# Six longer weight buffers and a sliding start for the split weights of the gate stage

## The chip, the core and the metric

The kernel runs on one core of one Trainium2 chip. The metric is the device time of one execution in microseconds (us), as the median of several executions. One more execution was taken by the hardware profiler; all rows below are from it. Engines are named as the profile names them: PE is the matrix engine (TensorE), PEld its weight loads, DVE the vector engine, ACT the scalar engine, POOL and SP the two others, of which SP issues most transfers.

## The reference, cut to what matters

```python
h = einsum('bsd,dn->bsn', x, w_in) + b_in      # x: 1 x 512 x 2048, w_in: 2048 x 11528, float32
# columns of h: three attention branches' q, k, v, z ... and three merge gates of 2048 columns each
br_i = einsum('bsw,wd->bsd', merged_heads(o_i) * silu(z_i), w_br_i)     # i = fox, swa, moba; w = 512
y = sum_i sigmoid(gate_i) * br_i
out = einsum('bsd,de->bse', y, w_out)
x = layer_norm(2 ** 0.25 * x + out, ln_g, ln_b)
```

## The kernel before, in words

Every float32 matrix product is done as three products of float32r parts: an operand `a` is split into `hi` (a rounded copy) and `lo` (what is left of it), and `hi*hi`, `hi*lo` and `lo*hi` are added up in PSUM. The input x is split once into `xh` and `xl`, which stay in the on-chip memory. The weights come through one stream of blocks of 128 x 512 numbers, in the order of the list `ids` of `weight_stream`. A block's kind is "h" (128 columns of the projection by a quarter of the 2048 inputs; four blocks make one column tile `t`), "v", "b" (a 512 x 128 piece of a branch matrix) or "o" (a piece of the output matrix). Two blocks come in one transfer into `raw`, which SP issues.

The main loop takes one block at each step `i`. It first calls `prepare(i + 2)`, which has ACT write the block's `hi`, and at once or a little later DVE its `lo` (`lower`), two steps ahead of their use. Then it calls the step of the block's kind, which issues its matmuls, and then the tasks that were set down for this step, in a written order. `tc.manual_schedule()` keeps the engines' instructions in the order in which the code issues them. A step of kind "h" or "b" issues 12 matmuls of 512 columns each. `hi` and `lo` have three buffers each in the pool `stage`, shared by all kinds of blocks; a buffer is written again when the matmuls of the block that was there are done.

The gate stage is the loop over `dt` from 0 to 15 in `weight_stream`: three column tiles for the next `dt` (12 blocks "h", 144 matmuls, `proj_step`), then three blocks "b" (36 matmuls, `branch_step`). Column tiles 33 to 80 are the 48 of the gates; the first three of them come before the loop and those of `dt` 1 to 15 inside it. In the blocks "h" and "b" the part `hi` or `lo` is the weight side of the matmul (128 columns of it are loaded into the array), and `xh`, `xl`, `ozh` or `ozl` the side that streams through. In the blocks "o" it is the other way round: `yh` or `yl` is loaded, and `hi` or `lo` streams.

Where things lie in the on-chip memory, in bytes from the start of a partition's row, by the built program (the part of 512 is what is left over from a multiple of 512):

| tiles | part of 512 |
|---|---|
| `hi`, `lo` (all six), `xh`, `xl`, `ozh`, `ozl`, `yh`, `yl` | 480 |
| `wh`, `wl` (the parts of the last eight blocks "o") | 416 |
| `qs`, `kh`, `kl`, `lt`, `pth`, `ptl`, `ident`, `tri`, `pair` (attention) | 160 |
| `vfox`, `vswa`, `vmoba` | 32 |

The matmuls take slices of them that begin at multiples of 128 or 256 numbers, 512 or 1024 bytes. So every place at which a matmul of this kernel begins to read, other than in the warm-up, has one of these four parts of 512, and all four are 32 past a multiple of 64.

Of the kernel before, what the change touches and what calls it, by code (L numbers as in the profile page):

```python
# [9 lines left out]
F32R = mybir.dt.float32r  # L10
# [3 lines left out]
P = 128  # L14
S = 512
# [5 lines left out]
ALPHA = 2.0 ** 0.25  # L21
LN_EPS = 1e-5
WARM = 7

FOX_Q, FOX_K, FOX_V, FOX_Z, FOX_F = 0, 512, 1024, 1536, 2048
SWA_Q, SWA_K, SWA_V, SWA_Z = 2056, 2568, 2696, 2824
# [27 lines left out]
def weight_stream():  # L54

    ids = []
    t = 0

    def proj(n):
        nonlocal t  # L60
        for _ in range(n):
            ids.extend(("h", t, c) for c in range(4))
            t += 1

    proj(12)
    proj(1)
    for p in range(4):
        proj(2)
        if p % 2 == 1:
            ids.extend(("v", p // 2, g) for g in range(8))  # L70
    proj(12)
    proj(3)
    for dt in range(KD):
        if dt + 1 < KD:
            proj(3)
        ids.extend(("b", dt, b) for b in range(3))
    ids.extend(("o", ec, k) for ec in range(4) for k in range(KD))
    return ids
# [3 lines left out]
def hybrid_kernel(ctx: ExitStack, tc: tile.TileContext, a: dict, out: bass.AP):  # L82
# [16 lines left out]
    def att_tile(name):  # L99
        return psum.tile([P, S], F32, tag="att", name=name, bufs=5)  # L100
# [6 lines left out]
    ids = weight_stream()  # L107
# [7 lines left out]
    def load(j):  # L115
        if 2 * j < len(ids) and j not in raws:
            raws[j] = stage.tile([P, 1024], F32, tag="raw", name="raw", bufs=raw_bufs)
            nc.sync.dma_start(raws[j], a["ws"][j])

    def prepare(i):  # L120

        if i >= len(ids) or i in parts:
            return None
        load(i // 2)
        raw = raws[i // 2][:, (i % 2) * S:(i % 2 + 1) * S]
        if i in held:
            hi, lo = held[i]
        else:
            hi = stage.tile([P, S], F32R, tag="hi", name="hi")
            lo = stage.tile([P, S], F32R, tag="lo", name="lo")  # L130
        parts[i] = (hi, lo)
        nc.scalar.activation(hi, raw, AF.Copy)  # L132

        def lower():
            nc.vector.tensor_sub(lo, raw, hi.bitcast(F32))  # L135
            for d in range(1, raw_bufs):
                load(i // 2 + d)

        return lower
# [48 lines left out]
    wacc = att_tile("warm")  # L188
    for n in range(WARM):
        nc.tensor.matmul(wacc, warm[:, :P], warm, start=True, stop=True)  # L190
# [89 lines left out]
    for n in range(2 * KD):  # L280
        if n + 4 < KD:
            load_x(n + 4)
        if n % 2 == 0 and n // 2 + 3 < KD:
            load_v(n // 2 + 3)
        if n + 2 < 2 * KD:
            prepare_v(n + 2)
        else:
            prepare(n + 2 - 2 * KD)()
        if n == KD:
            vacc[1] = [att_tile(f"vc{i}") for i in range(4)]  # L290
        v_step(n)
        if n == 4:
            nc.vector.tensor_scalar(nsink, sinkc, -1.0, None, op0=ALU.mult)
        if KD + 1 <= n < KD + 5:
            v_evac(0, n - KD - 1, fox_dests[0])
# [270 lines left out]
    box = {}  # L566
# [174 lines left out]
    for i in range(len(ids)):  # L741
        assert i in parts
        lower = prepare(i + 2)
        if lower:
            at(i, 2, lower)
        step[ids[i][0]](i)
        for _, _, f, args in sorted(tasks.pop(i, ()), key=lambda x: x[:2]):
            f(*args)
# [69 lines left out]
```

## Time and profile before

| | |
|---|---|
| median of 3 executions | 1400.79 us (1400.56 to 1402.41) |
| the profiled execution | 1399.89 us |
| its span, from the first to the last instruction | 1398.1 us |
| PE busy | 1377.4 us, 99% of the span, 6659 matmuls |
| PEld busy | 1162.8 us, 83% |
| DVE, ACT, POOL busy | 636.3, 556.8, 151.4 us |
| mean granted clock of PE | 0.995 of 2.4 GHz |

Busy times are shares of the span over all stages. PE's matmuls overlap in the profile: one of 512 columns is shown with 389 ns, while the next begins some 227 ns after it, so the distance from start to start (the pitch) is what counts, and it is read from stretches with a known number of matmuls.

### The profile page before, as it was taken

The page shows a single profiled execution, that of the slowest core. Times are in us where ns is not written, and L with a number is a line of the kernel's source. Part 1 is how long each engine was busy: PE and PEld are TensorE (multiplying, and loading weights), DVE is VectorE, ACT ScalarE, POOL GpSimd, SP SyncE. Part 2 cuts the span into 40 slices and gives each one's busy share as a digit, 9 for nine tenths or more (in the row PEclk, how much of TensorE's full clock was granted, in tenths as well). Part 3 has the DMA queues.
Part 4 walks back from the last instruction along what each step waited for, and adds up shares of the span by engine and source line. Part 5 has one row for each costly group of instructions (what it writes and reads, how often), then busy time and mean ns, then how long its engine had stood idle before and what let it go on. Part 6 is the DMA issues. An engine that isn't in the chain of part 4 may idle for free.

```text
span 1398.1 us, 17708 instructions
## 1 busy us (share of the span) xinstructions
PE 1377.4 (99%) x6659; PEld 1162.8 (83%) x6659; DVE 636.3 (46%) x1273; ACT 556.8 (40%) x1024; POOL 151.4 (11%) x216
## 2 busy tenths in 40 slices
PE   9999999999999999999999999999999999999994
PEld 8988888898988888888888888888888888888884
DVE  5466656545554555452333333233333323733348
ACT  5355566555545566642222222222222222422231
POOL 1002122332321222100000000000000000000006
PEclk9999999999999999999999999999999999999998
DMA  7333223222223222233332333323333332363323
GB/s 245 116 105 105 83 90 89 77 88 89 82 75 91 78 76 89 76 94 102 90 106 91 101 95 94 103 90 106 91 99 97 93 103 91 122 255 98 98 75 121
DMA packets 41157, 142.37 MB, mean 102 GB/s; under 512 B 4632, under 2 KB 5144, under 8 KB 40304
## 3 DMA queue, kind: packets, MB, share of 16 engines
q1 hardware_dynamic: 40048, 134.58, 30.8%
q0 software_dynamic: 1024, 6.67, 1.3%
q8 instruction: 52, 0.85, 0.3%
q14 instruction: 33, 0.27, 0.1%
HBM read 137.02 MB, written 4.21 MB: 101 GB/s over the span
## 4 chain that ended last, share of the span: by engine, by line
PE 96%; DVE 2%; DMA 1%; SPq 0%; issue 0%; ACT 0%; DVEq 0%; ACTq 0%
PE h L471 21%; PE h L473 21%; PE h L472 21%; PE br L599 9%; PE o L651 4%; PE o L650 4%; PE o L652 4%; PE o L417 2%; PE pt L398 2%; PE mv L490 1%; PE mv L492 1%; PE mv L493 1%; PE s L357 1%; PE s L356 1%; DMA xraw<-in_xT 1%; PE vc L274 1%
## 5 line engine op out<-in xcount | busy, mean ns | idle before, releaser
L132 ACT ACTIVATE hi<-raw 128x512 fp32r<-128x512 f32 x444 | 280.1, 631 | 711.1 <-PE h L472 426.8
L135 DVE TENSOR_TENSOR lo<-raw,hi 128x512 fp32r<-128x512 f32 x444 | 313.1, 706 | 540.9 <-ACT hi L132 532.7
L471 PE MATMUL h<-xh,hi 128*128 128x512 f32 x1296 | 507.4, 392 | 0.0
L473 PE MATMUL h<-xh,lo 128*128 128x512 f32 x1296 | 505.1, 390 | 0.1
L472 PE MATMUL h<-xl,hi 128*128 128x512 f32 x1296 | 505.2, 390 | 0.0
L473 PEld LDWEIGHTS h<-xh,lo 128*128 128x128 f32 x1296 | 243.3, 188 | 52.3 <-DVE lo L135 0.5
L471 PEld LDWEIGHTS h<-xh,hi 128*128 128x128 f32 x1296 | 243.4, 188 | 48.5
L472 PEld LDWEIGHTS h<-xl,hi 128*128 128x128 f32 x1296 | 243.5, 188 | 47.9
L393 POOL TENSOR_SCALAR lt<-lt,st 128x128 f32<-128x128 f32 (+2 forms) x96 | 71.2, 742 | 302.0 <-DVE st L392 300.0
L651 PE MATMUL o<-hi,yl 128*128 128x512 f32 (+1 forms) x232 | 88.6, 382 | 0.0
L650 PE MATMUL o<-hi,yh 128*128 128x512 f32 (+1 forms) x232 | 88.6, 382 | 0.0
L652 PE MATMUL o<-lo,yh 128*128 128x512 f32 (+1 forms) x232 | 88.6, 382 | 0.0
L599 PE MATMUL br<-ozh,hi 128*128 128x512 f32 x192 | 74.7, 389 | 0.0
L599 PE MATMUL br<-ozl,hi 128*128 128x512 f32 x192 | 74.7, 389 | 0.0
L599 PE MATMUL br<-ozh,lo 128*128 128x512 f32 x192 | 74.7, 389 | 0.0
L631 POOL DMA_DIRECT2D z<-in_xn x4 | 2.2, 556 | 625.3 <-DVE yl L104 625.3
L387 ACT ACTIVATE lt<-lt,st 128x128 f32<-128x128 f32 (+3 forms) x96 | 51.4, 535 | 23.7 <-DVE st L392 10.5
L650 PEld LDWEIGHTS o<-hi,yh 128*128 128x128 f32 x232 | 43.6, 188 | 8.6
L652 PEld LDWEIGHTS o<-lo,yh 128*128 128x128 f32 x232 | 43.6, 188 | 8.5
L651 PEld LDWEIGHTS o<-hi,yl 128*128 128x128 f32 x232 | 43.6, 188 | 8.3
L405 ACT ACTIVATE pth<-pt 128x128 fp32r<-128x128 f32 (+2 forms) x96 | 38.8, 404 | 14.8 <-PE pt L398 14.0
L409 DVE TENSOR_TENSOR ptl<-pt,pth 128x128 fp32r<-128x128 f32 (+2 forms) x96 | 43.2, 450 | 1.0 <-ACT pth L405 0.7
(156 smaller groups left out, 1426.9 us busy)
## 6 DMA issues: line engine op xcount, KB each, us to landing
raw<-in_ws SPq DMA_DIRECT2D x226, 512.0 KB, 3.6
rawv<-in_wv SPq DMA_DIRECT2D x15, 324.0 KB, 4.0
xraw<-in_xT SPq DMA_DIRECT2D x16, 256.0 KB, 6.3
z<-in_xn POOLq DMA_DIRECT2D x4, 1024.0 KB, 10.1
out<-z SPq DMA_DIRECT2D x7, 512.0 KB, 2.6
row<-forget_rows SPq DMA_DIRECT2D x8, 256.0 KB, 4.0
ln_gain<-in_ln_gain POOLq DMA_DIRECT2D x1, 1024.0 KB, 18.0
ln_bias<-in_ln_bias POOLq DMA_DIRECT2D x1, 1024.0 KB, 20.4
```

Of the source, the lines that this page charges most:

```text
L132: nc.scalar.activation(hi, raw, AF.Copy)
L135: nc.vector.tensor_sub(lo, raw, hi.bitcast(F32))
L387: nc.scalar.activation(full[:, :m], full[:, :m], AF.Exp, bias=st[:, 0:1], scale=-1.0, accum_out=st[:, 1:2])
L393: nc.gpsimd.tensor_scalar(lt, lt, st[:, 3:4], 1.0, op0=ALU.mult, op1=ALU.mult)
L409: nc.vector.tensor_sub(env["ptl"][:, c], u["pt"][:, :u["n"] // P], env["pth"][:, c].bitcast(F32))
L471: nc.tensor.matmul(accs[t], hi[:, cc], xh[:, k], start=(k == 0), stop=False)
L472: nc.tensor.matmul(accs[t], hi[:, cc], xl[:, k], start=False, stop=False)
L473: nc.tensor.matmul(accs[t], lo[:, cc], xh[:, k], start=False, stop=(k == KD - 1))
L599: nc.tensor.matmul(br, w[:, cc], o[:, 4 * b + kt], start=(kt == 0 and n == 0), stop=(kt == 3 and n == 2))
L650: nc.tensor.matmul(o, yb["h"][:, k, sl], hi, start=(k == 0), stop=False)
L651: nc.tensor.matmul(o, yb["l"][:, k, sl], hi, start=False, stop=False)
L652: nc.tensor.matmul(o, yb["h"][:, k, sl], lo, start=False, stop=(k == KD - 1))
```

## The change

From the column tile 39 on, that is in `dt` 2 to 15, the blocks "h" take their `hi` and `lo` from six buffers of their own (`ghi`, `glo`, three each) in the pool `mix`. Each is 640 numbers long, and the part of 512 numbers begins `o` numbers into it. `o` is the next number of `PLACES` after every three column tiles, so each of the 14 numbers holds for one `dt`, for 12 blocks and 144 matmuls. The blocks "b", "o" and the earlier blocks "h" keep the old buffers.

```diff
+PLACES = (0, 4, 8, 12, 16, 24, 32, 48, 64, 80, 96, 112, 124, 126)
...
         if i in held:
             hi, lo = held[i]
+        elif ids[i][0] == "h" and ids[i][1] >= 39:
+            o = PLACES[min((ids[i][1] - 39) // 3, len(PLACES) - 1)]
+            hi = box["mix"].tile([P, S + P], F32R, tag="ghi", name="ghi", bufs=3)[:, o:o + S]
+            lo = box["mix"].tile([P, S + P], F32R, tag="glo", name="glo", bufs=3)[:, o:o + S]
         else:
             hi = stage.tile([P, S], F32R, tag="hi", name="hi")
```

In the built program all six new buffers lie at the part 480 of 512, as the old ones do. With 4 bytes a number the 14 starts, as parts of 512, are 480, 496, 0, 16, 32, 64, 96, 160, 224, 288, 352, 416, 464 and 472. The two last `y` tiles (`dt` 14 and 15) move 15,360 bytes up in the pool, at the same part of 512.

Every engine has the same instructions in the same order before and after. What differs beside the addresses is what some of them wait for. On ACT, where the blocks of `dt` 2 begin and the first blocks "b" after them, each row being one instruction with the queues that it waits for (DVE and PE stand for the buffer's last users, DMAHW for the transfer into `raw`), it is before:

```order
L584 ACTIVATE sig<-h_6094,bT 128x512 [waits PE_49]
L132 ACTIVATE hi<-raw 128x512 [waits DVE_49,PE_49]
L132 ACTIVATE hi<-raw 128x512 [waits DMAHW4_49,DVE_49,PE_49]
L132 ACTIVATE hi<-raw 128x512 [waits DVE_49,PE_49]
L132 ACTIVATE hi<-raw 128x512 [waits DMAHW5_49,DVE_49,PE_49]
```

and with the change:

```order
L590 ACTIVATE sig<-h_6094,bT 128x512 [waits PE_49]
L138 ACTIVATE ghi<-raw 128x512
L138 ACTIVATE ghi<-raw 128x512 [waits DMAHW4_49]
L138 ACTIVATE ghi<-raw 128x512
L138 ACTIVATE ghi<-raw 128x512 [waits DMAHW5_49,DVE_49,PE_49]
```

The first three blocks "h" and the three blocks "b" of each of the 14 `dt` no longer wait for PE (84 instructions); the nine others of each `dt` wait as before.

## Rows read from the trace of the kernel before

**Rows 1.** The page: busy us (share of the span) and instructions; the chain that ended last.
```profile
PE 1377.4 (99%) x6659; PEld 1162.8 (83%) x6659; DVE 636.3 (46%) x1273; ACT 556.8 (40%) x1024; POOL 151.4 (11%) x216
...
PE 96%; DVE 2%; DMA 1%; SPq 0%; issue 0%; ACT 0%; DVEq 0%; ACTq 0%
```

**Rows 2.** All waits of PE in the whole span: us in total, times, longest.
```profile
PE warm L190 <- DVE warm L187: 1.5, 1, 1.5
PE va L272 <- ACT xh L103: 0.8, 1, 0.8
PE va L273 <- DVE xl L104: 0.6, 2, 0.3
```

**Rows 3.** The chain that ended last, in the gate stage: start, us, what.
```profile
618.01 8.16 PE br L599 x36
658.81 8.16 PE br L599 x36
...
1148.41 8.16 PE br L599 x36
1189.21 16.32 PE br L599 x72
```

**Rows 4.** Windows: one stretch of 144 projection matmuls (two more overlap its edges): engines, clock, DMA.
```profile
626.17:658.81 32.64, 32.64 (x146) 27.04 (x145) 9.62 (x14) 8.74 (x15) 0.00 (x0) 1.00 0.33 97
```

**Rows 5.** Groups by line and shape, 658.81 to 699.61: busy us, mean ns, idle before.
```profile
L473 PE MATMUL h<-xh,lo 128*128 128x512 f32 x49 | 19.1, 389 | 0.0
...
L471 PEld LDWEIGHTS h<-xh,hi 128*128 128x128 f32 x48 | 9.0, 188 | 1.9
```

**Rows 6.** Timeline of PE, 127.5 to 131, around an attention head's values: start, us.
```profile
128.33 0.39 PE L472 MATMUL h<-xl,hi 128*128 128x512 f32 x1
128.55 0.39 PE L473 MATMUL h<-xh,lo 128*128 128x512 f32 x1
128.78 0.39 PE L417 MATMUL o<-pth,vfox 128*128 128x512 f32 x1
129.01 0.39 PE L417 MATMUL o<-ptl,vfox 128*128 128x512 f32 x1
...
129.82 0.22 PE L417 MATMUL o<-pth,vfox 128*128 128x128 f32 x1
129.88 0.28 PE L417 MATMUL o<-ptl,vfox 128*128 128x128 f32 x1
129.99 0.41 PE L398 MATMUL pt<-ident,lt 128*128 128x128 f32 x2
```

**Rows 7.** The same stretch, weight loads.
```profile
128.56 0.19 PEld L417 LDWEIGHTS o<-pth,vfox 128*128 128x128 f32 x1
```

**Rows 8.** Groups by line and shape over the whole span, output blocks streaming `hi` or `wh`.
```profile
L650 PE MATMUL o<-hi,yh 128*128 128x512 f32 x216 | 84.1, 389 | 0.0
...
L650 PE MATMUL o<-wh,yh 128*128 128x512 f32 x24 | 9.5, 394 | 0.0
```

**Rows 9.** Timeline of PE near the end: first and last of 25 output matmuls streaming `wh` or `wl`.
```profile
1358.38 0.40 PE L651 MATMUL o<-wh,yl 128*128 128x512 f32 x1
...
1363.98 0.39 PE L651 MATMUL o<-wh,yl 128*128 128x512 f32 x1
```

**Rows 10.** Timelines of ACT and of DVE, 650 to 662; idle before, and what ended it.
```profile
650.46 0.63 ACT L132 ACTIVATE hi<-raw 128x512 fp32r<-128x512 f32 x1 [1.51 <-PE h L472]
653.18 0.63 ACT L132 ACTIVATE hi<-raw 128x512 fp32r<-128x512 f32 x1 [2.09 <-PE h L472]
...
651.13 0.69 DVE L135 TENSOR_TENSOR lo<-raw,hi 128x512 fp32r<-128x512 f32 x1 [2.03 <-ACT hi L132]
```

**Rows 11.** Waits of ACT, 620 to 1189: us in total, times, longest.
```profile
ACT hi L132 <- PE h L472: 315.8, 159, 2.1
ACT hi L132 <- PE br L599: 65.0, 35, 2.1
```

## The prediction

> **What bounds the kernel now.** I read the page first. PE is busy for 1377.4 us of the 1398.1 us span, and the chain that ended last runs over PE for 96% of it [rows 1]. So the next question is whether PE ever waits for data. The list of PE's waits has three entries, 2.9 us together, all of them at the start (the warm-up and the first value blocks) [rows 2]. In the gate stage PE waits for nothing. The chain shows how regular it is: a group of 36 branch matmuls begins every 40.80 us, from 618.01 to 1148.41, thirteen periods one after the other [rows 3]. Each group takes 8.16 us, 226.7 ns for a matmul. The other 32.64 us of a period are the 144 projection matmuls, again 226.7 ns each, at a granted clock of 1.00 [rows 3, 4]. The stage's time is therefore the number of matmuls times the pitch, and nothing else. An edit moves the time here only if it moves the pitch or makes PE wait. The first of the 14 stretches that the change touches is the one of rows 4.
>
> **The removed waits.** In each of the 14 periods six blocks get their buffer without waiting for PE, so ACT and DVE can write them earlier. ACT did wait long for PE, 315.8 us and 65.0 us in this stage [rows 11], but that was the pace PE set, not a delay to PE: PE's own list has no wait there [rows 2]. There is nothing to win: 0 us. A loss would need ACT or DVE to be late. A block's `hi` is written at 650.46 and its `lo` ends at 651.13 + 0.69 = 651.82 [rows 10]. The wait before that `hi` ended with PE's last use of the buffer, so the step in progress had just begun, and the block is used two steps later. Steps are 2.72 us apart (12 matmuls, and the distance of the two ACT rows), so it is needed at about 655.9 and has 4.1 us to spare. The instructions that now carry a wait of their own (the products of branch and gate on DVE) waited for the same matmuls before, through the write of `lo` ahead of them in DVE's queue. Cost 0.
>
> **Writing to the new places.** ACT and DVE write 168 `hi` and 168 `lo` at the 14 starts. No row shows a write to a place off a multiple of 32 bytes, so I bound it: below, no change; above, twice the time, another 0.63 us on ACT and 0.69 us on DVE [rows 10]. Both together, 1.3 us, lie within the 4.1 us, so both ends cost 0. Without that cover, 14 x 12 blocks at 1.3 us would be 220 us, but the cover would have to shrink by two thirds first.
>
> **Loading weights from the new places.** This is the one term that can count, since it multiplies 14 x 144 = 2016 matmuls. A weight load is shown with 188 ns [rows 5] and runs while the matmul before it streams, so it has the 226.7 ns of the pitch. How much of this does it need? Two matmuls of 128 columns in the attention stage start at 129.82 and 129.88, and the next instruction starts at 129.99, each with a load of its own [rows 6]: 85 ns each on average, at most 110 ns. So a load that took twice as long (at most 220 ns of throughput) would still fit under the pitch. Lower bound 0, and 0 also for a load up to twice as slow.
>
> Loads may also disturb the stream that runs beside them. Addresses do matter for the streaming side: the output matmuls that stream `wh` from the part 416 of 512 are shown with 394 ns, those that stream `hi` from 480 with 389 ns, with the same weights' places [rows 8]. Read by starts, 24 pitches take 1363.98 - 1358.38 = 5.60 us, 233.3 ns each [rows 9], against 226.7 ns. A place can thus cost a step of 6.7 ns. But the change leaves the stream (`xh`, `xl` at 480) where it is and moves the loaded side. The trace has a few cases of just that. Where a projection matmul is followed by one of an attention head, the load that runs beside the projection matmul comes from `vfox`, at the part 32, rather than from 480 [rows 7]. That projection matmul starts at 128.55 and the next at 128.78, after one from 128.33 to 128.55 with a load from 480 [rows 6]: 0.22 and 0.23 us, the same to the view's 0.01 us. A step of 6.7 ns would hardly show in that one pair, which is why this evidence is good and not final. I take 0.
>
> Eight of the 14 starts (480, 32, 96, 160, 224, 288, 352, 416) are 32 past a multiple of 64, as every operand of the kernel before. Two (0 and 64) are multiples of 64, and four (496, 16, 464, 472) are off every multiple of 32: no row shows a matmul that reads at such a place, so for these six I have only the bound of one step, 6.7 ns, either way, and keep it for the range.
>
> **The sum.** 0 + 0 + 0: the profiled execution's 1399.89 us would stay. It lies 0.9 us (0.06%) below the median of the three runs, and I forecast that median, 1400.8 us. A measurement of this kernel can tell about 0.2% (2.8 us) from no change.
>
> **Rivals.**
>
> *Slower: starts off 32 bytes cost a step.* Place: the periods of 496, 16, 464 and 472. Price: 4 x 144 x 6.7 ns = 3.8 us, 1404.6 us. For it: the step exists on the streaming side [rows 8, 9], and a row of weights that straddles one more unit of the memory needs one more read. Against it: the extra read falls on the load, which has over 100 ns to spare. It decides from 4.9 ns a matmul on (2.8 us over 576). If instead all 13 moved starts cost a step, it is 13 x 144 x 6.7 ns = 12.5 us, 1413.3 us; the pair above speaks against it. Worse than a step would need a load of more than twice its time.
>
> *Faster: the start at 480 costs PE something, and other starts give it back.* 512 columns at 2.4 GHz are 213.3 ns, so 13.3 ns of each pitch are not streaming. If part of this came from loading at 480, the six unseen kinds of start could return a step each: 6 x 144 x 6.7 ns = 5.8 us, 1395.0 us; all 13 would return 12.5 us, 1388.3 us. Only the two multiples of 64 would be 1.9 us, too little to measure. For it: the excess is there, and it has the size of two steps. Against it: with a load from 32 the pitch was not shorter [rows 6].
>
> The Trainium skill ("TensorE: Matmul & The Clock Gate", section "Back-to-back issue gap") gives the warm gap as N/2.4 + 2.5 ns, 215.8 ns for 512 columns, which is 10.9 ns under what the row here shows. By that rule, taken as what well-placed operands reach, 13 moved starts could give back 13 x 144 x 10.9 ns = 20 us (an estimate from that page); the trace does not bear this out, since no 512-column matmul in it comes near that gap, from any of the four parts of 512.
>
> *The change does not do what it says.* The starts are not spread from a multiple of 512 but from 480 past one; the list of places already takes this in. It changes which starts are odd ones, not the sum.
>
> **How the numbers follow.** No measurable change 0.70: the load is hidden and eight of 14 starts are of the kind known; this holds the case of the two multiples of 64 alone. Slower 0.17: four starts cost a step 0.12, more than that 0.05. Faster 0.13: up to six starts return a step 0.09, more 0.04. The range reaches to both measured-step cases and a little beyond, 1395 to 1405 us, and leaves out about 1 in 10 by these cases, and some more for their sizes.
>
> **What would show it.** In the profile after, the branch groups should still begin 40.80 us apart in all 14 periods, and the projection groups show 389 ns. Since each period has one start, a period that is longer by 144 steps (0.96 us) names the start that costs; a shorter one names a start that pays. ACT's waits for PE in this stage should fall by some 84 entries with no new wait on PE. I am wrong if periods differ from each other, above all those of 0, 64 and of the four odd starts, or if a wait appears on PE.

## The result and the profile after

| | before | with the change |
|---|---|---|
| median | 1400.67 us (1400.27 to 1402.41) | 1408.63 us (1408.20 to 1408.97) |
| span of the profiled execution | 1398.1 us | 1406.5 us |

The change makes the kernel slower: ratio 1.0054, 95% interval 1.0037 to 1.0072. The forecast was no change, with a range that ended at 1405 us.

The page of the changed kernel: busy time by engine, and four groups by line.

```profile
PE 1386.4 (99%) x6659; PEld 1164.4 (83%) x6659; DVE 633.7 (45%) x1273; ACT 549.1 (39%) x1024; POOL 151.4 (11%) x216
...
L141 DVE TENSOR_TENSOR glo<-raw,ghi 128x512 fp32r<-128x512 f32 x168 | 116.1, 691 | 343.8 <-ACT ghi L138 343.8
...
L477 PE MATMUL h<-xh,ghi 128*128 128x512 f32 x672 | 264.2, 393 | 0.0
...
L138 ACT ACTIVATE ghi<-raw 128x512 fp32r<-128x512 f32 x168 | 103.0, 630 | 341.2 <-PE h L478 341.2
L477 PEld LDWEIGHTS h<-xh,ghi 128*128 128x128 f32 x672 | 126.4, 188 | 28.9
```

PE is busy 9.0 us longer with the same 6659 matmuls. The writes to the odd places take 630 ns on ACT and 691 ns on DVE, as before. A weight load is shown with 188 ns, as in [rows 5]. Only the matmuls beside these loads are longer: 393 ns on the mean instead of 389. PE's list of waits again has three entries, all at the start:

```profile
PE warm L196 <- DVE warm L193: 1.5, 1, 1.5
PE va L278 <- ACT xh L105: 0.7, 1, 0.7
PE va L279 <- DVE xl L106: 0.3, 1, 0.3
```

ACT's list, from 620 to 1198 us, is shorter than in [rows 11], where `hi` waits 194 times for PE:

```profile
ACT ghi L138 <- PE h L478: 341.2, 126, 8.5
ACT sig L590 <- PE h L479: 88.8, 14, 6.5
```

None of this holds PE up, so the time is in the pitch. The chain that ended last shows in which groups (start, us, what), against the even 40.80 us of [rows 3]:

```profile
618.14 8.16 PE br L605 x36
658.94 8.16 PE br L605 x36
699.74 8.17 PE br L605 x36
741.50 8.17 PE br L605 x36
783.26 8.16 PE br L605 x36
825.02 8.19 PE br L605 x36
866.95 8.17 PE br L605 x36
908.58 8.16 PE br L605 x36
949.71 8.16 PE br L605 x36
990.50 8.16 PE br L605 x36
1032.26 8.20 PE br L605 x36
1073.93 8.16 PE br L605 x36
1115.05 8.16 PE br L605 x36
1155.85 8.17 PE br L605 x36
1197.62 16.34 PE br L605 x72
```

From one row's end to the next row's start lie the 144 projection matmuls with one of the 14 starts, in the order of the list: the first from 626.30 to 658.94 (480), the third from 707.91 to 741.50 (0), and so on. 33.59 us / 144 = 233.3 ns. From the first row to the last it is 579.48 us, against 571.20 us in [rows 3]: 8.28 us of the 8.4 us by which the span grew. The windows of the groups with the starts 0 and 32 show all else as in [rows 4], the clock at 1.00 too:

```profile
707.91:741.50 33.59, 33.59 (x145) 27.05 (x145) 9.43 (x14) 8.42 (x14) 0.00 (x0) 1.00 0.34 110
791.42:825.02 33.60, 33.60 (x146) 27.07 (x145) 9.41 (x14) 8.41 (x14) 0.00 (x0) 1.00 0.36 110
```

By start (part of 512), from the starts of the matmuls in the trace, the pitch in ns:

| 480 | 496 | 0 | 16 | 32 | 64 | 96 | 160 | 224 | 288 | 352 | 416 | 464 | 472 |
|---|---|---|---|---|---|---|---|---|---|---|---|---|---|
| 226.7 | 226.7 | 233.3 | 233.3 | 233.3 | 234.2 | 232.4 | 228.9 | 226.7 | 233.3 | 232.4 | 228.9 | 226.7 | 233.3 |

Pairs that lie 256 apart (32 and 288, 96 and 352, 160 and 416, 224 and 480) agree to 0.02 ns. The pitch hangs on the start within 256 bytes, and not on whether it is a multiple of 32 or 64. Times 144, the excess over 226.67 ns adds up to 8.17 us.

### The profile page after: what moved, and what is told of

Same layout as the page of the kernel before. It is cut to its first block, busy times and chain, and to the rows that moved or that the text cites. A ratio compares the mean times of both kernels' runs of the same rounds, so it can differ in the third digit from the quotient of the medians.

```text
span 1406.5 us, 17608 instructions
## 1 busy us (share of the span) xinstructions
PE 1386.4 (99%) x6659; PEld 1164.4 (83%) x6659; DVE 633.7 (45%) x1273; ACT 549.1 (39%) x1024; POOL 151.4 (11%) x216
## 4 chain that ended last, share of the span: by engine, by line
PE 96%; DVE 2%; DMA 0%; issue 0%; ACT 0%; SPq 0%; DVEq 0%; ACTq 0%
PE h L477 21%; PE h L478 21%; PE h L479 21%; PE br L605 9%; PE o L657 4%; PE o L656 4%; PE o L658 4%; PE o L423 2%; PE pt L404 2%; PE mv L496 1%; PE mv L498 1%; PE mv L499 1%; PE s L363 1%; PE s L362 1%; PE vc L279 1%; PE vc L278 1%
## 5 line engine op out<-in xcount | busy, mean ns | idle before, releaser
L478 PE MATMUL h<-xl,ghi 128*128 128x512 f32 x672 | 264.4, 393 | 0.0
L477 PE MATMUL h<-xh,ghi 128*128 128x512 f32 x672 | 264.2, 393 | 0.0
L479 PE MATMUL h<-xh,glo 128*128 128x512 f32 x672 | 263.8, 393 | 0.0
L477 PE MATMUL h<-xh,hi 128*128 128x512 f32 x624 | 246.1, 394 | 0.0
L478 PE MATMUL h<-xl,hi 128*128 128x512 f32 x624 | 243.8, 391 | 0.0
L479 PE MATMUL h<-xh,lo 128*128 128x512 f32 x624 | 243.7, 391 | 0.1
L477 PEld LDWEIGHTS h<-xh,ghi 128*128 128x128 f32 x672 | 126.4, 188 | 28.9
L479 PEld LDWEIGHTS h<-xh,glo 128*128 128x128 f32 x672 | 126.4, 188 | 28.8
L478 PEld LDWEIGHTS h<-xl,ghi 128*128 128x128 f32 x672 | 126.4, 188 | 28.2
L477 PEld LDWEIGHTS h<-xh,hi 128*128 128x128 f32 x624 | 117.2, 188 | 22.3
```

What stands on the lines that cost most here:

```text
L477: nc.tensor.matmul(accs[t], hi[:, cc], xh[:, k], start=(k == 0), stop=False)
L478: nc.tensor.matmul(accs[t], hi[:, cc], xl[:, k], start=False, stop=False)
L479: nc.tensor.matmul(accs[t], lo[:, cc], xh[:, k], start=False, stop=(k == KD - 1))
```

## The experiments

All are edits of the changed kernel unless said otherwise. A run for which no ratio is given is a single execution; the pitches of its groups are what counts there. "Distance" is the start of the loaded weights less the start of the streamed operand, as part of 256. With the change `xh` and `xl` begin at 224 of 256, so the start 480 has distance 0, and the start 32 has distance 64.

**The buffers without the sliding start.**
```diff
-PLACES = (0, 4, 8, 12, 16, 24, 32, 48, 64, 80, 96, 112, 124, 126)
+PLACES = (0,) * 14
```


> The six new buffers stay, but all 14 starts are o = 0, the part 480 of 512. If the time hangs on where the loaded weights start (A), every projection group of the gate stage is back at 144 x 226.7 ns = 32.64 us and the time is that of before, 1400.7 us. If the new buffers themselves, their place in the memory or the waits that changed cost the time (B), it stays near 1408.6 us.

1400.29 us against 1400.71 us, ratio 0.9997 (0.9988 to 1.0006). The branch groups stand 40.80 us apart again (start and us):

```profile
618.16 8.16 PE br L605 x36
658.96 8.16 PE br L605 x36
```

So the new buffers, their place far up in the memory, the moved `y` tiles and the waits that went away are worth nothing that shows, as A had it; B falls.

**One slow start for all.** `PLACES = (24,) * 14`.

> All 14 starts are o = 24, the part 64 of 512, the start whose group was the longest with the change (33.73 us, 234.2 ns a matmul). If each start has its own price whatever came before it (A), the 2016 matmuls cost 7.57 ns each more than before: 15.3 us, 1416.0 us. If the price comes from changing the start, or depends on the group before (C), it is well below that, by the 14 changes no more than the 8 us of the change.

1415.28 us, ratio 1.0105 (1.0088 to 1.0122); A had 1416.0, C no more than 1409. All 14 groups have 234.2 ns (from branch group to branch group, start and us):

```profile
617.92 8.16 PE br L605 x36
659.81 8.16 PE br L605 x36
701.70 8.16 PE br L605 x36
```

The first gap is 659.81 - 626.08 = 33.73 us. A start has a price of its own and keeps it.

**The streamed side moved by 64 bytes.** `xh` and `xl` get a longer tile each and begin 16 numbers into it; the outputs' `yh` and `yl`, in the same two tiles, begin at 0.
```diff
-    xh = keep.tile([P, KD, S], F32R, tag="bigh", name="xh")
-    xl = keep.tile([P, KD, S], F32R, tag="bigl", name="xl")
+    def big(tag, name, o):
+        flat = keep.tile([P, KD * S + 64], F32R, tag=tag, name=name)
+        return flat[:, o:o + KD * S].rearrange("p (k s) -> p k s", s=S)
+
+    xh, xl = big("bigh", "xh", 16), big("bigl", "xl", 16)
...
+            yb["h"], yb["l"] = big("bigh", "yh", 0), big("bigl", "yl", 0)
```


> The changed kernel with its 14 starts, and the streamed xh and xl begin 64 bytes later: at the part 32 instead of 224 of 256. If the price hangs on the loaded side's start alone (theory L), or on the writes to it, the 14 groups show the same pitches as with the change: 226.7 ns at 480, 496, 224, 352+112 and 233.3 at 0, 16, 32, 288, 472. If it hangs on the distance from the streamed side's start to the loaded side's within 256 bytes (theory D), the pitches move by 64 bytes: 226.7 ns at 32 and 288 (distance 0) and 16 (distance 240), 233.3 at 64, 96 and 352 (distances 32, 64), 232 to 234 at 160 and 416 (distance 128), 228.9 at 480 and 224 (distance 192).

Its chain, from the branch group before the start 16 to the one after the start 64:

```profile
743.73 8.20 PE br L608 x36
784.60 8.17 PE br L608 x36
825.45 8.18 PE br L608 x36
867.21 8.17 PE br L608 x36
```

The group at 16 takes 784.60 - 751.93 = 32.67 us (226.9 ns; it was 233.3), the one at 32 takes 825.45 - 792.77 = 32.68 us (227.0; it was 233.3), the one at 64 takes 33.58 us (233.2). The group at 480, the good place until now, has 229.0 ns. The fast starts moved along with the stream, as D said, with nothing changed in the loads or in the writes of ACT and DVE. L falls. The total, 1409.55 us, tells little of this: the 14 starts for the most part exchanged their prices.

**More distances, and two repeated.** `PLACES = (20, 28, 36, 40, 44, 52, 56, 60, 1, 2, 3, 6, 24, 48)`.

> The changed kernel with other numbers in the list: o = 20, 28, 36, 40, 44, 52, 56, 60 (new multiples of 16 bytes: the parts 48, 80, 112, 128, 144, 176, 192, 208 of 256), 1, 2, 3, 6 (4, 8, 12 and 24 bytes past 480), and again 24 and 48. By both theories the multiples of 16 fall on the curve of the change: 233.3 at 48, 232 to 235 from 80 to 144, below 228.9 from 176 on, 226.7 at 208; 24 and 48 repeat 234.2 and 228.9 ns at another place in the order. If an odd start costs by itself, as 472 seems to, the starts 4, 8, 12 and 24 bytes past 480 show 233 ns although 480 and 496 show 226.7; if only the distance counts, they show 226.7.

The total is 1408.99 us. 24 and 48 repeat 234.2 and 228.9 ns at another place in the order. The expected curve was missed at five of the eight new multiples of 16, though, as it is no smooth one: distance 144 has 226.7 ns between 128 with 232.4 and 160 with 233.3; 208 has 231.8 and 240 has 226.7. Neither of the two values named for starts off 16 bytes, 233 for all or 226.7 for all, came out: such a start has no price as such, since 12 bytes past 480 shows 226.7 ns, but 4, 8 and 24 past show 232.4, 230.7 and 231.1.

**Only `lo` at the odd starts.**
```diff
-            hi = box["mix"].tile([P, S + P], F32R, tag="ghi", name="ghi", bufs=3)[:, o:o + S]
+            hi = box["mix"].tile([P, S + P], F32R, tag="ghi", name="ghi", bufs=3)[:, :S]
```


> The changed kernel with its 14 starts for lo alone; hi stays at o = 0. Only one load of three then comes from another distance. If the matmul that streams while such a load runs pays (D1), the one from xl and hi (line 478) is longer at the bad starts, by about 7 ns on the mean of its pitch, and the two others stay at 227 ns: a third of the 8.2 us, 2.7 us, 1403.4 us. If the matmul that uses the weights so loaded pays (D2), it is the one from lo (line 479). If the price needs a run of loads at the same distance (D3), as a settled rhythm would, all three stay at 227 ns and the time at 1400.7 us.

1407.22 us: none of the three. One odd load of three keeps most of the price. The group with `lo` at the start 32 stands between these rows of the chain:

```profile
783.33 8.16 PE br L605 x36
824.77 8.17 PE br L605 x36
```

824.77 - 791.49 = 33.28 us, 231.1 ns a matmul against 233.3 with both parts there, and from the starts in the trace the three kinds of matmul have 228, 229 and 236 ns. Which of the three pays most changes with the start: at 0 they have 232, 239 and 229 ns, at 64 233, 230 and 233. At 160 and 416 (distance 192) the one odd load costs even more than all three did, 231.1 against 228.9 ns. So the price can't be put on one matmul of the three, nor added up load by load; it looks like a rhythm of the row of matmuls as a whole.

**The kernel before with the streamed side at other places** (the edit of the 64 bytes, on the kernel before, with 28, 4 and 60 numbers for 16): an attempt to keep the gate stage and to speed up the value stages.

> The kernel before with xh and xl 112 bytes later. The projection groups load at distance 144, which showed 226.7 ns: no change there, 32.64 us a group. The 384 matmuls of 256 columns that load xh or xl and stream hi or lo (120.8 ns on the mean) and the 384 of 324 columns then work at distance 112. If the price goes by distance there too, they move: 113 to 122 ns for 256 columns, at best 384 x 7 ns = 2.7 us less (1398 us), at worst 1.5 us and for 324 columns 3 us more. If only 512-column matmuls have it, 1400.7 us.

> The kernel before with xh and xl 16 bytes later. Projection groups at distance 240 (226.7 ns, 32.64 us a group); the matmuls of 256 and 324 columns at distance 16. By distance: 113 to 122 ns for 256 columns, the time between 1398 and 1402 us; if only 512-column matmuls have the price, 1400.7 us.

> The kernel before with xh and xl 240 bytes later, the mirror of 16 bytes later: projection groups at distance 16 (226.7 ns), matmuls of 256 and 324 columns at distance 240. By distance: 113 to 122 ns for 256 columns, the time between 1398 and 1402 us; if only 512-column matmuls have the price, 1400.7 us.

1415.29, 1416.09 and 1423.18 us: ratios 1.0104 (1.0089 to 1.0120), 1.0110 (1.0093 to 1.0127) and 1.0162 (1.0146 to 1.0177). Their projection groups have 231.0, 231.7 and 233.3 ns in place of 226.7, so the distances 144, 240 and 16 weren't safe ones. The value matmuls of 256 columns gained little or nothing (121.0, 119.7 and 119.9 ns on the mean, 120.8 before). The rule of distance as stated fell here, and the next four runs ask what it lacks.

**The stream at two more multiples of 32.** The edit of the 64 bytes with 32 numbers (128 bytes), and with 8 numbers (32 bytes) and `PLACES = (8, 12, 16, 20, 24, 32, 40, 44, 48, 56, 60, 0, 4, 10)`.

> The changed kernel with its 14 starts, and xh and xl 128 bytes later, at the part 96 of 256 (32 past a multiple of 64, as in all runs in which the distance alone gave the pitch). If the distance within 256 bytes decides for such a stream, the pitches are known beforehand: 226.7 ns at 96 and 352 (distance 0) and 496 (144), 228.9 at 32 and 288 (192), 230.0 at 16 (176), 232.4 at 480 and 224 (128), 233.3 at 64 (224), at 160 and 416 (64) and at 464 (112). If the loaded side's start decides, the 14 are those of the change.

> The changed kernel with xh and xl 32 bytes later, at a multiple of 256, and other starts in the list, at the distances 0, 16, 32, 48, 64, 96, 128, 144, 160, 192, 208, 224, 240 and 8. If the distance alone decides, the pitches are, in this order, 226.7, 226.7, 233.3, 233.3, 233.3, 234.2, 232.4, 226.7, unknown, 228.9, 231.8, 233.3, 226.7 and 230.7 ns. If the stream's own start within 64 bytes counts as well, as the runs with xh and xl 16, 112 and 240 bytes later speak for, several of the 14 differ by more than 1 ns; a pitch below 226.7 ns, should there be one, would be a place for a faster kernel.

Pitches in ns by distance, from the starts of the matmuls, for the runs in which the stream begins at a multiple of 32 ("entered slow" is the run below):

| distance | change, stream at 224 | further starts, 224 | +64 bytes, at 32 | +128 bytes, at 96 | +32 bytes, at 0 | entered slow, 224 |
|---|---|---|---|---|---|---|
| 0 | 226.7 | | 227.0 | 226.7 | 226.9 | 226.9 |
| 32 | 233.3 | | 233.3 | | 233.2 | |
| 64 | 233.3 | | 233.4 | 233.3 | 233.4 | |
| 96 | 234.2 | 234.2 | | | 234.2 | |
| 128 | 232.4 | | 232.4 | 233.3 | 233.3 | |
| 192 | 228.9 | 228.9 | 229.0 | 229.0 | 228.9 | |
| 208 | | 231.8 | 231.8 | | 231.9 | |
| 224 | | 233.3 | 233.3 | 233.3 | 233.4 | |
| 12 | | 226.7 | | | | 233.3 |
| 16 | 226.7 | | | | 233.4 | 233.3 |
| 144 | | 226.7 | | 233.3 | 233.3 | 233.3 |
| 240 | 226.7 | 226.7 | 226.9 | | 228.4 | 228.4 |

Seven of the twelve are firm within 0.3 ns at each of these streams at which they were run, 128 within 1 ns. So are four that the table leaves out, each seen in two or three of these runs: 48, 112 and 160 (233.3 to 233.4 ns) and 176 (230.0). 12, 16, 144 and 240 have two values each. The slow one at 144, with the stream at 96, stands between these rows of its chain (711.12 - 677.52 = 33.60 us, 233.3 ns a matmul):

```profile
669.35 8.17 PE br L608 x36
711.12 8.19 PE br L608 x36
```

The totals, 1418.58 and 1419.58 us, are higher than that of the change for the most part because the earlier projection matmuls leave distance 0 there too: the first of the 14 groups begins 9.5 and 8.6 us later (635.60 and 634.74 us against 626.14).

**The groups entered out of a slow rhythm.** `PLACES = (0, 4, 36, 60, 0, 4, 36, 60, 3, 0, 4, 36, 60, 3)`, all 226.7 ns until now, and the branch blocks from slow starts of the same buffers, while `xh` and `xl` stay where they were:
```diff
-        elif ids[i][0] == "h" and ids[i][1] >= 39:
-            o = PLACES[min((ids[i][1] - 39) // 3, len(PLACES) - 1)]
+        elif ids[i][0] == "h" and ids[i][1] >= 39 or ids[i][0] == "b" and ids[i][1] >= 1:
+            o = (24 if ids[i][1] < 8 else 16) if ids[i][0] == "b" else PLACES[min((ids[i][1] - 39) // 3, 13)]
```


> The changed kernel with the starts o = 0, 4, 36, 60 and 3 alone, the distances 0, 16, 144, 240 and 12, all of which showed 226.7 ns with xh and xl where they were, and the branch blocks of dt 1 to 15 loaded from a bad start (distance 96 for dt 1 to 7, 64 after), so that a projection group is entered out of a slow rhythm. Where xh and xl were moved, the distances 16, 144 and 240 gave 227 to 233 ns. If that came from the rhythm in which the group is entered (E), some of the groups at 16, 144 and 240 stay slow here, 228 to 233 ns for the whole group, while distance 0 falls back to 226.7 ns. If it came from the stream's own start (S), every projection group is back at 226.7 ns after a few matmuls, within 0.3 ns on the mean. The 540 branch matmuls of these dt should cost 7.6 and 6.7 ns each, 3.9 us together: 1404.6 us under S, up to 1412 us under E.

1412.84 us, which is E (its sum ended at 1412). The chain's first branch group still has the old buffers, the others the slow start:

```profile
618.45 8.16 PE br L605 x36
659.25 8.43 PE br L605 x36
701.28 8.43 PE br L605 x36
743.31 8.43 PE br L605 x36
784.62 8.43 PE br L605 x36
825.74 8.43 PE br L605 x36
```

Between them: distance 0, entered as always, 659.25 - 626.61 = 32.64 us; then 16 with 33.60 us, 144 with 33.60, 240 with 32.88, and again 0 with 825.74 - 793.05 = 32.69. The same starts with the same stream had 32.64 us each when the branch matmuls before them ran fast. At 12, 16, 144 and 240 a row of matmuls stays in the rhythm in which it was entered, for all 144; at distance 0 it falls back to 226.7 ns within some ten matmuls. The values found here for 16, 144 and 240, 233.3, 233.3 and 228.4, are those of the two runs with the stream at 96 and at 0. That speaks for one cause, but doesn't prove it: in those two runs the branch matmuls before such a group ran at 226.7 ns, and the slow rhythm begins at the border, where load and stream change over (at 144 with the stream at 96, the first two matmuls of the group have 232 and 237 ns). That the border sets the rhythm there is argued, not shown, and it doesn't always: with the stream at 32 the group at 240 has up to 239 ns in its first matmuls and is back at 226.7 after four of them.

**The stream off a multiple of 32.** The edit of the 64 bytes with 4 numbers (16 bytes), and `PLACES = (4, 12, 20, 28, 52, 56, 48, 60, 36, 0, 8, 6, 16, 24)`.

> The changed kernel with xh and xl 16 bytes later, at the part 240 of 256 (48 past a multiple of 64), and the starts at the distances 0, 32, 64, 96, 192, 208, 176, 224, 128, 240, 16, 8, 48 and 80. If the distance decides wherever the stream begins, and only a few distances (16, 144, 240) also hang on how the group is entered, the pitches are, in this order, 226.7 to 227.0, 233.3, 233.3, 234.2, 228.9, 231.8, 230.0, 233.3, 232.4 to 233.3, for 240 the 231.7 of the run with the same starts, 226.7 or 233.4, 230.7, 233.3 and 232.0 ns. If the stream's own start within 64 bytes counts too, the firm ones (0, 32, 64, 96, 192, 208, 176) differ from this by more than 1 ns.

The firm distances are firm no more: 0 has 230.0 ns, 32 has 227.0, 64 has 228.9, 96 has 227.0, 192 has 226.8, 208 has 233.3 and 176 has 231.1. Two rows of its chain, around the distance 32 (706.82 - 674.13 = 32.69 us):

```profile
665.94 8.19 PE br L608 x36
706.82 8.21 PE br L608 x36
```

So the stream's own start seems to count as well, and the runs with 28, 4 and 60 numbers, whose streams begin at 80, 240 and 208 of 256, all off a multiple of 32, stand on another curve than the table's. One point of it was seen twice: distance 240 with the stream at 240 has 231.65 ns here and in the run with 4 numbers. The total is 1415.91 us. In all twelve runs no projection group went below 226.7 ns.

## Why the prediction was wrong, point by point

- **The removed waits, 0 us: right.** With the buffers alone the ratio is 0.9997. PE's list has no new wait.
- **Writing to the new places, 0 us: right,** at 630 and 691 ns not even the cover was needed.
- **Loading weights from the new places, 0 us: wrong, the step that failed.** The working asked first whether a load gets longer and whether the pitch has room for it. It doesn't get longer (188 ns), so the room wasn't needed. It asked next whether a load disturbs the stream beside it, and took 0 for that without a row that could show it: this is the term that failed. With loads of the same length the pitch goes by where they start against the running stream. The price is 8.17 us, an average of 4.1 ns on 2016 matmuls. A step of 6.7 ns was named, from [rows 8, 9], but put down to the streamed side, which the change leaves alone. Those rows were themselves a case of distance 64: `yh` loaded from 224 of 256, `wh` streamed from 160. They show 233.3 ns, and so does the change at distance 64.
- **The evidence that outvoted it was one pair.** In [rows 6, 7] a load at distance 64 ran beside one matmul and the pitch stayed at 0.23 us. That was the first matmul of a new distance, and the changed kernel shows what such a one is worth. Its timeline where the branch matmuls end and the group with the start 32, the same distance 64, begins:

```profile
790.81 0.39 PE L605 MATMUL br<-ozl,hi 128*128 128x512 f32 x1
791.04 0.39 PE L605 MATMUL br<-ozh,lo 128*128 128x512 f32 x1
791.26 0.40 PE L477 MATMUL h<-xh,ghi 128*128 128x512 f32 x1
791.50 0.39 PE L478 MATMUL h<-xl,ghi 128*128 128x512 f32 x1
791.73 0.40 PE L479 MATMUL h<-xh,glo 128*128 128x512 f32 x1
791.96 0.39 PE L477 MATMUL h<-xh,ghi 128*128 128x512 f32 x1
```

  The first load from the new start runs beside the matmul of 791.04, and the next begins 0.22 us later, as if nothing had changed; the price begins one later, with 0.24 and 0.23 in turn (236 and 230 or 231 ns in the trace). The prediction called the pair good and not final, and then took its value for the sum.
- **The rivals.** "All 13 moved starts cost a step" was on record with 12.5 us and a part of the 0.05. The sign was right, but ten starts cost, and only five of them the step of 6.7 ns (0, 16, 32, 288, 472); the others cost 2.2 (160, 416), 5.8 (96, 352) and 7.6 ns (64). That last one is more than a step with a load of the same 188 ns, where the prediction asked for a load of twice its time. The rival of the four odd starts was half right: 16 and 472 cost, 496 and 464 cost nothing, which the reason given for it, a row across one more unit of the memory, doesn't explain. 0, 64, 32, 96, 160, 288, 352 and 416 cost, among them six that were taken as the kind known. Being 32 past a multiple of 64 was not what made a start good.
- **The gain did not come.** No start went below 226.7 ns. The Trainium skill's gap of N/2.4 + 2.5 ns ("TensorE: Matmul & The Clock Gate", section "Back-to-back issue gap"), which the section gives for an isolated matmul, a condition that the prediction left out, was not reached by any group of 512-column matmuls in any run here: 226.7 ns is the least, against 215.8. The Trainium skill says on the same page, in Part 2 ("What happens when you issue a matmul", step 1), that loading the next weights does not steal read bandwidth from the running matmul. The trace differs in effect: with the same load time the matmul's pitch goes from 226.7 to 234.2 ns with the load's start alone, and the measurement decides; whether it is bandwidth that is lost, no run shows.
- **What would show it: right in the main.** The periods differ by start, and each names its price. ACT's waits for PE fell by 54, from 194 to 140, and not by some 84: those of the writes of `hi` fell by 68, and 14 new ones stand at the gates' sigmoid.

What stays open: by what way the start of a load changes the pitch. The runs show that it hangs on both starts, with a period of 256 bytes in the loaded one, and at some distances on the rhythm before. The curve for streams off a multiple of 32 was seen at one place only, and whether it too hangs on the entry wasn't tried.

## What to carry to other kernels

Where PE runs matmuls of this kind back to back (float32r, 128 x 128 loads, 512 columns; no other shape was settled here), look up at which part of 256 bytes the loaded and the streamed operand begin, and give them the same one, at a multiple of 32: such groups had 226.7 to 227.0 ns with the stream at 0, 32, 96 and 224 of 256, and 230.0 ns with the stream at 240. A tile that begins 16 bytes further can be enough to lose it (231.7 ns in the second run on the kernel before), and here that is worth up to 3% of the stage (41.89 us a period with every start at distance 96, against 40.80). A pitch must be read from a settled row of tens of matmuls at one pair of addresses, not from a single pair. When a row in the profile shows that addresses matter, ask which of the two operands it speaks of before using it for one.

## What the hardware showed unexpectedly

At four distances (12, 16, 144, 240) the same matmuls with both operands at the same parts of 256 bytes ran at 226.7 ns or at 233.3 ns (228.4 for 240), for the whole group of 144, by how they were entered, the stream at 224 throughout. And one load of three at a bad distance kept 4.4 of the 6.7 ns that three of three cost (231.1 against 233.3 ns, from 226.7), while at distance 192 it cost more than three of three (231.1 against 228.9 ns).
